# Rows written to DRAM in copies, one of four one-hots on another engine, and two sums in one operation

## The chip, the cores and the metric

The kernel runs on one core of a Trainium2 chip. The metric is the device time of one execution in microseconds (us); lower is better. Before the change three runs gave a median of 2655.18 us (2654.83 to 2657.31). The profile is of one more execution of the same program.

The engines are named as in the profile: PE (TensorE, matrix products), PEld (its weight loads), DVE (VectorE), ACT (ScalarE), POOL (GpSimd) and SP, which here issues transfers only. PEclk is TensorE's granted clock, 1.00 for 2.4 GHz and 0.50 for 1.2 GHz.

## The reference, cut to what matters

One decoder layer for 264 token columns: 256 of a prompt and 8 samples. Mixers give x1; then a layer with 16384 single-neuron experts (PEER) and a second normalization follow:

```python
x1 = layer_norm(ALPHA * x + mix @ w_out, ln1_g, ln1_b)
x2 = layer_norm(ALPHA * x1 + peer(x1, peer_wq, peer_keys1, peer_keys2, peer_u, peer_v), ln2_g, ln2_b)
y = x2 + jax.nn.sigmoid(x2 @ ple_gate_w) * (p @ ple_proj_w)

# in peer, for each token: 8 heads, top 16 of 128x128 key pairs, then
hid = jax.nn.gelu(jnp.einsum('td,thkd->thk', xb, u_tab[ib]), approximate=False)
coef = gb * hid
out = jnp.einsum('thk,thkd->td', coef, v_tab[ib])
```

## The kernel before, in words

**Two ways through the experts.** For 208 of the 264 columns the kernel multiplies with all experts: 128 blocks of `uT` (the u stage, `pair_block` with `u_evac`), a gate matrix that is zero where a token did not choose an expert, and then 8 x 16 blocks of `vP` (the v stage). The other 56 columns take only the expert rows that they chose (`sparse_experts`): 112 indirect gathers of 128 rows of 2048 floats, 56 from `uR` and 56 from `vR`, in groups of 32, 16 and 8 tokens (`GR`). In a group of n tokens each of the 128 partitions serves one token, and each token has 128/n partitions.

**Weights.** Every weight half (128 x 1024 floats, 512 KB) is loaded by SP into one of 5 buffers `w`, rounded by ACT into `whi` (line 146), and its remainder is made by DVE as `wlo` (line 147). Both have 4 buffers and are made 3 halves ahead of PE. A half in the u or v stage is 8 pairs of products (lines 273 or 276, and 274).

**What sets the order.** The program is written out in ticks, one for each half. After each half's products a background scheduler runs tasks as far as a budget allows, and functions that were deferred to this tick. So each engine's order is fixed when the program is built; on the chip each engine works through its own list and waits for semaphores. SP's list has the loads of `w`, the sends of indices (line 1165) and the writes of finished gate blocks `g_d` (line 1205), in one order.

**The rows x1 of the sparse tokens.** `token_rows` transposes the 56 columns of x1 into 56 rows of 8 KB in `xr`, and POOL writes them to DRAM as `x1_d` (line 1227). Before each group `replicate` (lines 1247 to 1251) reads them back so that each partition has the row of its token: one transfer of 1 MB, whose source is written as 128/n copies outermost (with step 0), then n rows, then 2048 floats. DVE multiplies the gathered `uR` rows with it (line 1289); later the same tile collects the `vR` rows (lines 1297, 1299).

**The gate matrix.** `gates` makes for each 4 tokens two one-hot tiles: `o1` by POOL (line 1200, four operations of 128 x 128) and `o2` by ACT. Six ticks later PE multiplies them (line 1213) and ACT copies the product into the gate block `gs`; after 32 tokens SP writes the block to DRAM. A new group of four tokens comes every 3 ticks. On POOL's list the one-hots stand between the gathers (line 1237). A gather waits for the buffer `ug` of the last but one, thus for DVE.

**The second norm.** In class `Norm`, `gather` takes each finished block of 208 columns: DVE subtracts a pilot mean, ACT scales it into `h` and squares it into a block of its own, DVE makes `l` and adds the values (line 847) and the squares (line 848) to two sums. `rest` does the same for the 56 sparse columns, with sums into the last columns of the same two tiles. `stats` multiplies both sums with a constant matrix to sum over partitions (lines 896 and 898).

Of the kernel before, what the change touches and what calls it, by code (L numbers as in the profile page):

```python
# [10 lines left out]
F = mybir.dt.float32  # L11
# [41 lines left out]
def hybrid_step(ctx: ExitStack, tc: tile.TileContext, xT, pT, w_in, w_dt, w_bs, w_bc, w_o, w_q, w_pg, w_pp,  # L53
# [748 lines left out]
    class Norm:  # L802
        def __init__(self, g_base, b_base, name, new, w=T):
            self.g, self.b, self.name, self.new = g_base, b_base, name, new
            self.w = w
            self.h, self.l = [], []
            self.gb = []
            src = cpar[:, g_base:g_base + 32].rearrange("p (a j) -> p j a", a=2)
            h = cpool.tile([128, 16, 2], R, name=name + "gbh")
            l = cpool.tile([128, 16, 2], R, name=name + "gbl")  # L810
            ac.copy(h, src)
            ve.tensor_tensor(l, src, h.bitcast(F), OP.subtract)
            self.gb = [h.bitcast(F), l.bitcast(F)]
            self.s0 = None
            self.c = None
            self.d = []
            self.acc = None
# [8 lines left out]
        def gather(self, s):  # L826
            j = len(self.d)
            w = self.w
            ve.tensor_tensor(s[:, :w], s[:, :w], self.c[:, :w], OP.subtract)
            self.d.append(s)  # L830
            h, l = self.new(self.name)
            q = block("dsq")

            def on_act():
                ac.activation(h[:, :w], s[:, :w], AF.Copy, scale=col(self.g, j))
                ac.activation(q[:, :w], s[:, :w], AF.Square)
                gp.tensor_copy(h[:, T:], self.gb[0][:, j])  # L837
                gp.tensor_copy(l[:, T:], self.gb[1][:, j])
                if j == 0:
                    a = block("da")  # L840
                    gp.tensor_copy(a[:, :w], s[:, :w])
                    self.acc = (a, q)

            def on_dve():
                ve.scalar_tensor_tensor(l[:, :w], s[:, :w], col(self.g, j), h[:, :w].bitcast(F), OP.mult, OP.subtract)
                if j:
                    ve.tensor_tensor(self.acc[0][:, :w], self.acc[0][:, :w], s[:, :w], OP.add)
                    ve.tensor_tensor(self.acc[1][:, :w], self.acc[1][:, :w], q[:, :w], OP.add)

            self.h.append(h)  # L850
            self.l.append(l)
            soon(on_act)
            soon(on_dve)

        def rest(self, xs, sq):
# [9 lines left out]
            yield ("w", 1)  # L865
            ac.activation(sq, xs, AF.Square)
            ve.tensor_reduce(self.acc[0][:, w:T], xs.rearrange("p j t -> p t j"), AX.X, OP.add)
            yield 1.0
            yield ("w", 1)
            ve.tensor_reduce(self.acc[1][:, w:T], sq.rearrange("p j t -> p t j"), AX.X, OP.add)  # L870
            yield 1.0
            for j in range(16):
                while len(self.h) <= j:
# [3 lines left out]
                gp.tensor_copy(self.d[j][:, w:T], x)  # L877
# [14 lines left out]
        def stats(self):  # L892
# [3 lines left out]
            te.matmul(pm[:, :T], o2048, self.acc[0], start=True, stop=True)  # L896
            pv = bank("pv")
            te.matmul(pv[:, :T], o2048, self.acc[1], start=True, stop=True)
# [253 lines left out]
    x1_d = dram.tile([NSP, D], F, name="x1_d")  # L1152
# [34 lines left out]
    def gates(t0, n):  # L1187
        oh = P["oh"]
        grid = Grid()
        for tt in range(t0, t0 + n, 4):  # L1190
# [7 lines left out]
            for q in range(4):  # L1198
                c = slice(tt + q, tt + q + 1)
                gp.tensor_scalar(o1[:, q], iot, slot[0][:, c], slot[2][:, c], OP.is_equal, OP.mult)  # L1200
# [15 lines left out]
    def token_rows():  # L1216
# [10 lines left out]
        gp.dma_start(out=x1_d, in_=xr[:NSP])  # L1227

    def sparse_experts():
# [16 lines left out]
        def replicate(g):  # L1246
            k0, n = GR[g]
            t = lp.tile([128, D], F, name="x1s", tag="x1s", bufs=2)
            gp.dma_start(out=t, in_=bass.AP(tensor=x1_d.tensor, offset=x1_d.offset + k0 * D,
                                            ap=[[0, 128 // n], [D, n], [1, D]]))  # L1250
# [146 lines left out]
    def v_evac(c, db):  # L1397
        def f(ps):
# [5 lines left out]
            if c == ECH - 1:  # L1404
                ve.tensor_tensor(a[:, :TD], a[:, :TD], a[:, TD:], OP.add)
                n2.add(a[:, :T])
# [208 lines left out]
```

## Time and profile before

| | |
|---|---|
| median of three runs | 2655.18 us |
| the profiled execution, its own time | 2653.27 us |
| its span, first to last instruction | 2651.0 us |
| PE busy | 2572.5 us (97%) |
| DVE busy | 2032.7 us (77%) |
| ACT busy | 1426.3 us (54%) |
| POOL busy | 723.4 us (27%) |
| moved by DMA | 692.61 MB, mean 261 GB/s |

The busy share is a mean over the whole span. The u stage lies between about 1140 and 1800 us, the v stage from there to about 2540 us. POOL's share is small in all but high while the gate matrix is made (1290 to 1790 us). A view of stretches (windows) gives for each engine the busy time and, in brackets, how many instructions began; the number of products that PE began in a stretch, against a stretch of the same work where it had no gap, tells how much was lost to gaps and to a lower clock together.

### The profile page before, as it was taken

Reading aid. Unit: us, or ns where it says so; the run is one execution under the profiler, and the core shown is the slowest. Engines: PE = TensorE matmul, PEld = TensorE weight load, DVE = VectorE, ACT = ScalarE, POOL = GpSimd, SP = SyncE. Lnnn points to the kernel's source line nnn. Section 1 sums busy time; section 2 is a strip of 40 time slices with the busy share of each in tenths; the row PEclk is TensorE's granted clock in tenths of the full one; section 3 lists DMA queues with packets and bytes.
Section 4 is the critical chain, followed back from the end, with each engine's and each line's share of the span. In section 5 each row is a group of like instructions: output and inputs, shape, how many; then the busy total and the mean of one; then the engine's idle time right before and its main releaser. Section 6 shows DMA issues by size and latency. Waiting matters only on the chain. (4 is left out here: it accounts for less than half of the span.)

```text
span 2651.0 us, 49042 instructions
## 1 busy us (share of the span) xinstructions
PE 2572.5 (97%) x18985; PEld 2536.4 (96%) x18985; DVE 2032.7 (77%) x3271; ACT 1426.3 (54%) x2170; POOL 723.4 (27%) x775
## 2 busy tenths in 40 slices
PE   8999999999999999999979999799999999999999
PEld 8999999999999999999979899799999999999999
DVE  8899965556445567899878667577889989989986
ACT  5665533454344445654667777675544444445563
POOL 2232200000000010100449689772232233322210
PEclk9999999999999999999989999899999999999999
DMA  6798755555555555566778999899999999999664
GB/s 232 221 294 275 242 169 180 181 173 184 182 180 181 181 178 176 178 198 206 215 249 331 343 341 338 281 353 386 362 348 362 377 355 366 371 358 369 206 196 133
DMA packets 204410, 692.61 MB, mean 261 GB/s; under 512 B 23976, under 2 KB 61528, under 8 KB 188504
## 3 DMA queue, kind: packets, MB, share of 16 engines
q1 hardware_dynamic: 156512, 509.13, 57.5%
q0 software_dynamic: 29648, 162.29, 16.5%
q10 hardware_dynamic: 18016, 18.06, 2.0%
q8 instruction: 148, 2.42, 0.4%
q14 instruction: 86, 0.70, 0.1%
HBM read 649.46 MB, written 39.92 MB: 260 GB/s over the span
## 5 line engine op out<-in xcount | busy, mean ns | idle before, releaser
L147 DVE TENSOR_TENSOR wlo<-w,whi 128x1024 fp32r<-128x1024 f32 x916 | 1117.1, 1225 | 461.8 <-ACT whi L146 449.2
L146 ACT CAST whi<-w 128x1024 fp32r<-128x1024 f32 x916 | 958.9, 1049 | 799.4 <-PE mm L238 289.6
L273 PE MATMUL mm<-x,whi 128*128 128x416 f32 x1920 | 601.7, 373 | 19.0 <-ACT whi L146 19.0
L273 PE MATMUL mm<-co,whi 128*128 128x416 f32 x1920 | 588.4, 367 | 0.9 <-ACT whi L146 0.9
L239 PE MATMUL mm<-x,wlo 128*128 128x264 f32 x1920 | 549.9, 286 | 2.8 <-DVE wlo L147 2.8
L237 PE MATMUL mm<-x,whi 128*128 128x264 f32 x1920 | 549.9, 286 | 1.0 <-ACT whi L146 1.0
L238 PE MATMUL mm<-x,whi 128*128 128x264 f32 x1920 | 547.4, 285 | 0.0
L274 PE MATMUL mm<-x,wlo 128*128 128x208 f32 x2048 | 516.5, 262 | 27.2 <-DVE wlo L147 26.8
L274 PE MATMUL mm<-co,wlo 128*128 128x208 f32 x2048 | 514.4, 261 | 7.9 <-DVE wlo L147 7.6
L274 PEld LDWEIGHTS mm<-x,wlo 128*128 128x128 f32 x2048 | 395.4, 193 | 34.8 <-DVE wlo L147 34.1
L274 PEld LDWEIGHTS mm<-co,wlo 128*128 128x128 f32 x2048 | 390.4, 191 | 15.2 <-DVE wlo L147 14.5
L273 PEld LDWEIGHTS mm<-x,whi 128*128 128x128 f32 x1920 | 366.0, 191 | 24.7 <-ACT whi L146 20.0
L237 PEld LDWEIGHTS mm<-x,whi 128*128 128x128 f32 x1920 | 363.5, 189 | 2.7 <-issue 1.4
L273 PEld LDWEIGHTS mm<-co,whi 128*128 128x128 f32 x1920 | 360.9, 188 | 5.1 <-ACT whi L146 1.8
L239 PEld LDWEIGHTS mm<-x,wlo 128*128 128x128 f32 x1920 | 362.6, 189 | 3.3 <-DVE wlo L147 3.2
L238 PEld LDWEIGHTS mm<-x,whi 128*128 128x128 f32 x1920 | 363.6, 189 | 0.0
L1200 POOL TENSOR_SCALAR o<-iot,slot,slot 128x128 f32<-128x128 f32 x208 | 311.7, 1505 | 3.6 <-ACT slot L1142 1.9
L1237 POOL DMA_INDIRECT ug<-vR,sidx x56 | 101.8, 1818 | 300.8 <-DVE x1s L1299 253.5
L1237 POOL DMA_INDIRECT ug<-uR,sidx x56 | 85.5, 1527 | 227.0 <-DVE ug L1289 202.6
L1299 DVE SCALAR_TENSOR_TENSOR x1s<-ug,scf,x1s 128x2048 f32<-128x2048 f32 x53 | 124.3, 2345 | 16.7 <-DMA ug<-vR,sidx 16.6
L837 POOL CAST r1h<-r1gbh 128x2 fp32r<-128x2 f32 x16 | 5.3, 329 | 476.2 <-PE mm L239 476.2
L1289 DVE SCALAR_TENSOR_TENSOR ug<-ug,x1s 128x2048 f32<-128x2048 f32 x56 | 127.8, 2282 | 3.8 <-DMA ug<-uR,sidx 3.8
(360 smaller groups left out, 3913.2 us busy)
## 6 DMA issues: line engine op xcount, KB each, us to landing
w<-uT SPq DMA_DIRECT2D x256, 512.0 KB
w<-vP SPq DMA_DIRECT2D x256, 512.0 KB
w<-w_in SPq DMA_DIRECT2D x240, 512.0 KB
w<-w_bc SPq DMA_DIRECT2D x32, 512.0 KB
w<-w_bs SPq DMA_DIRECT2D x32, 512.0 KB
w<-w_o SPq DMA_DIRECT2D x32, 512.0 KB
w<-w_q SPq DMA_DIRECT2D x32, 512.0 KB
w<-w_pg SPq DMA_DIRECT2D x32, 512.0 KB
```

Source lines behind the costliest of these rows:

```text
L146: ac.copy(hi, w)
L147: ve.tensor_tensor(lo, w, hi.bitcast(F), OP.subtract)
L237: te.matmul(ps, wh, xh[kb], start=(first and q == 0), stop=False)
L238: te.matmul(ps, wh, xl[kb], start=False, stop=False)
L239: te.matmul(ps, wl, xh[kb], start=False, stop=(last and q == n - 1))
L273: te.matmul(ps, hi[:, ws], xp[kb], start=(kb == 0), stop=False)
L274: te.matmul(ps[:, :TD], lo[:, ws], xp[kb][:, :TD], start=False, stop=False)
L837: gp.tensor_copy(h[:, T:], self.gb[0][:, j])
L1200: gp.tensor_scalar(o1[:, q], iot, slot[0][:, c], slot[2][:, c], OP.is_equal, OP.mult)
L1237: gp.indirect_dma_start(out=t, out_offset=None, in_=tab, in_offset=bass.IndirectOffsetOnAxis(ap=sidx[:, c:c + 1], axis=0))
L1289: ve.scalar_tensor_tensor(t, t, 1.0, x1s, OP.mult, OP.mult, accum_out=shid[:, c:c + 1])
L1299: ve.scalar_tensor_tensor(x1s, t, scf[:, c:c + 1], x1s, OP.mult, OP.add)
```

## The change

Three edits, in four places of the code.

- **Rows in copies.** `x1_d` becomes three DRAM tensors of 128 rows, one for each group. `token_rows` issues three writes, of 32, 16 and 8 rows, each row 4, 8 or 16 times, into the order in which the partitions need them. `replicate` reads 128 rows in their order.
- **One-hots.** Of the four operations for `o1` POOL makes three and DVE the fourth.
- **Second norm.** The squares go into the second half of the same 416 wide tile as the values (where `w < T`, thus in the second norm only), and one operation adds both to one sum. The 56 sparse columns have a sum tile of their own, so that `stats` has four products in place of two. `rest` counts blocks whose operations have been written to the lists (`self.n`) where it counted tiles.

```diff
--- before.py
+++ after.py
@@ -814,6 +814,7 @@
             self.s0 = None
             self.c = None
             self.d = []
+            self.n = 0
             self.acc = None
 
         def pilot(self):
@@ -824,28 +825,39 @@
             self.gather(self.s0)
 
         def gather(self, s):
+
             j = len(self.d)
             w = self.w
+            beside = w < T
             ve.tensor_tensor(s[:, :w], s[:, :w], self.c[:, :w], OP.subtract)
-            self.d.append(s)
+            self.d.append(s[:, :T])
             h, l = self.new(self.name)
-            q = block("dsq")
+            q = s[:, w:2 * w] if beside else block("dsq")
 
             def on_act():
                 ac.activation(h[:, :w], s[:, :w], AF.Copy, scale=col(self.g, j))
-                ac.activation(q[:, :w], s[:, :w], AF.Square)
+                ac.activation(q, s[:, :w], AF.Square)
                 gp.tensor_copy(h[:, T:], self.gb[0][:, j])
                 gp.tensor_copy(l[:, T:], self.gb[1][:, j])
                 if j == 0:
-                    a = block("da")
-                    gp.tensor_copy(a[:, :w], s[:, :w])
-                    self.acc = (a, q)
+                    if beside:
+                        a = lp.tile([128, 2, w], F, name="da", tag="as", bufs=2)
+                        gp.tensor_copy(a.rearrange("p a t -> p (a t)"), s)
+                        self.acc = [(a[:, 0], a[:, 1])]
+                        self.both = a.rearrange("p a t -> p (a t)")
+                    else:
+                        a = block("da")
+                        gp.tensor_copy(a, s)
+                        self.acc = [(a, q)]
 
             def on_dve():
                 ve.scalar_tensor_tensor(l[:, :w], s[:, :w], col(self.g, j), h[:, :w].bitcast(F), OP.mult, OP.subtract)
-                if j:
-                    ve.tensor_tensor(self.acc[0][:, :w], self.acc[0][:, :w], s[:, :w], OP.add)
-                    ve.tensor_tensor(self.acc[1][:, :w], self.acc[1][:, :w], q[:, :w], OP.add)
+                if j and beside:
+                    ve.tensor_tensor(self.both, self.both, s, OP.add)
+                elif j:
+                    for a, x in zip(self.acc[0], (s, q)):
+                        ve.tensor_tensor(a, a, x, OP.add)
+                self.n += 1
 
             self.h.append(h)
             self.l.append(l)
@@ -863,18 +875,20 @@
             ve.tensor_tensor(xs, xs, c[:, None, :].to_broadcast([128, 16, n]), OP.subtract)
             yield 1.0
             yield ("w", 1)
+            a = block("da")[:, 0:2 * n].rearrange("p (a t) -> p a t", a=2)
             ac.activation(sq, xs, AF.Square)
-            ve.tensor_reduce(self.acc[0][:, w:T], xs.rearrange("p j t -> p t j"), AX.X, OP.add)
+            ve.tensor_reduce(a[:, 0], xs.rearrange("p j t -> p t j"), AX.X, OP.add)
             yield 1.0
             yield ("w", 1)
-            ve.tensor_reduce(self.acc[1][:, w:T], sq.rearrange("p j t -> p t j"), AX.X, OP.add)
+            ve.tensor_reduce(a[:, 1], sq.rearrange("p j t -> p t j"), AX.X, OP.add)
+            self.acc.append((a[:, 0], a[:, 1]))
             yield 1.0
             for j in range(16):
-                while len(self.h) <= j:
+                while self.n <= j:
                     yield ("w", 1)
                 h, l, x = self.h[j][:, w:T], self.l[j][:, w:T], xs[:, j]
                 ac.activation(h, x, AF.Copy, scale=col(self.g, j))
-                gp.tensor_copy(self.d[j][:, w:T], x)
+                gp.tensor_copy(self.d[j][:, w:], x)
 
                 def low(h=h, l=l, x=x, j=j):
                     ve.scalar_tensor_tensor(l, x, col(self.g, j), h.bitcast(F), OP.mult, OP.subtract)
@@ -893,9 +907,13 @@
 
             yield ("w", 1)
             pm = bank("pm")
-            te.matmul(pm[:, :T], o2048, self.acc[0], start=True, stop=True)
             pv = bank("pv")
-            te.matmul(pv[:, :T], o2048, self.acc[1], start=True, stop=True)
+            for k, p in enumerate((pm, pv)):
+                t = 0
+                for a in self.acc:
+                    n = a[k].shape[-1]
+                    te.matmul(p[:, t:t + n], o2048, a[k], start=True, stop=True)
+                    t += n
             m = block("m")
             ac.copy(m, pm[:, :T])
             m2 = block("m2")
@@ -1149,7 +1167,7 @@
 
     sx_d = [dram.tile([128, n], U32, name=f"sx{g}_d") for g, (_, n) in enumerate(GR)]
     sg_d = [dram.tile([128, n], F, name=f"sg{g}_d") for g, (_, n) in enumerate(GR)]
-    x1_d = dram.tile([NSP, D], F, name="x1_d")
+    x1_d = [dram.tile([128, D], F, name=f"x1{g}_d") for g in range(len(GR))]
 
     def send(sel, t, nh):
 
@@ -1197,7 +1215,7 @@
             o2 = oh.tile([128, 4, 128], F, name="o2", tag="o2", bufs=3)
             for q in range(4):
                 c = slice(tt + q, tt + q + 1)
-                gp.tensor_scalar(o1[:, q], iot, slot[0][:, c], slot[2][:, c], OP.is_equal, OP.mult)
+                (gp if q < 3 else ve).tensor_scalar(o1[:, q], iot, slot[0][:, c], slot[2][:, c], OP.is_equal, OP.mult)
                 ac.activation(o2[:, q], iot, AF.Abs, bias=slot[1][:, c], scale=-1.0)
             ac.activation(o2, o2, AF.Relu, bias=1.0, scale=-1.0)
             defer(6, lambda o1=o1, o2=o2, gs=gs, q0=q0: g_mm(o1, o2, gs, q0))
@@ -1224,7 +1242,9 @@
                 te.transpose(ps[:NSP, q * 128:(q + 1) * 128], x1sp[:, 4 * b + q], ident)
             ac.copy(xr[:NSP, b * 512:(b + 1) * 512], ps[:NSP])
             yield ("w", 1)
-        gp.dma_start(out=x1_d, in_=xr[:NSP])
+        for g, (k0, n) in enumerate(GR):
+            gp.dma_start(out=x1_d[g].rearrange("(q n) d -> n q d", n=n),
+                         in_=xr[k0:k0 + n, None, :].to_broadcast([n, 128 // n, D]))
 
     def sparse_experts():
         jobs = [(tab, k0, n, c) for k0, n in GR for tab in (uR, vR) for c in range(k0, k0 + n)]
@@ -1244,10 +1264,8 @@
             gp.dma_start(out=scf[:, k0:k0 + n], in_=sg_d[g])
 
         def replicate(g):
-            k0, n = GR[g]
             t = lp.tile([128, D], F, name="x1s", tag="x1s", bufs=2)
-            gp.dma_start(out=t, in_=bass.AP(tensor=x1_d.tensor, offset=x1_d.offset + k0 * D,
-                                            ap=[[0, 128 // n], [D, n], [1, D]]))
+            gp.dma_start(out=t, in_=x1_d[g])
             return t
 
         def folded(g, acc):
@@ -1403,7 +1421,7 @@
                 ve.tensor_tensor(a, ps, a, OP.add)
             if c == ECH - 1:
                 ve.tensor_tensor(a[:, :TD], a[:, :TD], a[:, TD:], OP.add)
-                n2.add(a[:, :T])
+                n2.add(a)
         return f
 
     def finish():
```

The three places in the engines' lists, first POOL's at the start of the gate matrix and of the first sparse group. In the names, `o_` and a number is an `o1` tile, `x_d` the rows in DRAM, `x1s` the tile of replicated rows, `ug` a gathered tile. Before:

```order
L1227 DMA x_d<-xr 56x2048
L1165 DMA sx_d<-ix_16006 32x4x32
...
L1200 TENSOR_SCALAR o_16101<-iot,slot_14373,slot_14375 128x128 x4
L1200 TENSOR_SCALAR o_16209<-iot,slot_14373,slot_14375 128x128 x4
L1200 TENSOR_SCALAR o_16320<-iot,slot_14373,slot_14375 128x128 x4
L1243 DMA sidx<-sx_d 128x32
L1244 DMA scf<-sg_d 128x32
L1237 DMA ug<-uR,sidx 128x2048
L1249 DMA x1s<-x_d 128x1x2048
L1200 TENSOR_SCALAR o_16446<-iot,slot_14373,slot_14375 128x128 x4
```

The same place of POOL's list after the change:

```order
L1246 DMA x_d<-xr 32x4x2048
L1246 DMA x_d<-xr 16x8x2048
L1246 DMA x_d<-xr 8x16x2048
L1183 DMA sx_d<-ix_16010 32x4x32
...
L1218 TENSOR_SCALAR o_16105<-iot,slot_14375,slot_14377 128x128 x3
L1218 TENSOR_SCALAR o_16213<-iot,slot_14375,slot_14377 128x128 x3
L1218 TENSOR_SCALAR o_16324<-iot,slot_14375,slot_14377 128x128 x3
L1263 DMA sidx<-sx_d 128x32
L1264 DMA scf<-sg_d 128x32
L1257 DMA ug<-uR,sidx 128x2048
L1268 DMA x1s<-x_d 128x2048
L1218 TENSOR_SCALAR o_16450<-iot,slot_14375,slot_14377 128x128 x3
```

Three writes stand where one stood, nine one-hots where twelve stood ahead of the index loads and the first gather, and the read of the rows keeps its place.

DVE's list in the middle of the u stage (`as` is a finished u block), before:

```order
L1289 SCALAR_TENSOR_TENSOR ug,shid<-ug,x1s 128x2048
L147 TENSOR_TENSOR wlo<-w,whi 128x1024
L1333 TENSOR_TENSOR as<-mm,as 128x208
L147 TENSOR_TENSOR wlo<-w,whi 128x1024 x2
L1333 TENSOR_TENSOR as<-mm,as 128x208
```

and after:

```order
L1307 SCALAR_TENSOR_TENSOR ug,shid<-ug,x1s 128x2048
L147 TENSOR_TENSOR wlo<-w,whi 128x1024
L1351 TENSOR_TENSOR as<-mm,as 128x208
L147 TENSOR_TENSOR wlo<-w,whi 128x1024
L1218 TENSOR_SCALAR o_19759<-iot,slot_14375,slot_14377 128x128
L147 TENSOR_TENSOR wlo<-w,whi 128x1024
```

One one-hot has come between two remainders `wlo`; there are 52 such places. From the fourth on, this operation has a wait for POOL, because its tile was last written by POOL three groups of tokens earlier.

DVE's list in the second norm, before:

```order
L845 SCALAR_TENSOR_TENSOR r_28010<-acc,cpar,r_28010 128x208
L847 TENSOR_TENSOR da<-da,acc 128x208
L848 TENSOR_TENSOR dsq<-dsq 128x208
L147 TENSOR_TENSOR wlo<-w,whi 128x1024
L1403 TENSOR_TENSOR acc<-mm,acc 128x416
```

and after:

```order
L854 SCALAR_TENSOR_TENSOR r_28014<-acc,cpar,r_28014 128x208
L856 TENSOR_TENSOR da<-da,acc 128x416
L147 TENSOR_TENSOR wlo<-w,whi 128x1024
L1421 TENSOR_TENSOR acc<-mm,acc 128x416
L1423 TENSOR_TENSOR acc<-acc 128x208
```

Two sums of 208 columns have become one of 416; nothing else moved there. SP's list is the same row by row, and PE's differs only in the four products of `stats`.

## Rows read from the trace of the kernel before

**Rows 1.** The page's 40 slices of the span (66 us each): PE's busy tenths and the granted clock.

```profile
PE   8999999999999999999979999799999999999999
PEclk9999999999999999999989999899999999999999
```

**Rows 2.** Stretches around the first sparse group; columns: stretch, its length, then busy us and number begun for PE, PEld, DVE, ACT, POOL, the granted clock, the busy share of the DMA engines and GB/s.

```profile
1282.00:1318.00 36.00, 36.00 (x246) 35.69 (x244) 31.11 (x80) 27.36 (x46) 27.39 (x26) 1.00 0.65 206
1306.00:1312.00 6.00, 6.00 (x43) 5.96 (x43) 5.66 (x18) 5.55 (x10) 5.01 (x6) 1.00 0.11 32
1318.00:1345.00 27.00, 8.88 (x43) 7.89 (x43) 7.56 (x29) 6.62 (x13) 3.27 (x4) 0.62 0.84 193
1318.00:1336.00 18.00, 2.66 (x16) 2.21 (x15) 1.75 (x9) 0.00 (x0) 3.27 (x4) 0.65 1.00 201
1354.00:1363.00 9.00, 7.26 (x38) 6.88 (x38) 8.79 (x16) 4.88 (x11) 1.87 (x2) 0.81 0.57 181
```

**Rows 3.** POOL in order of time around the first sparse group; columns: start, duration, line, operation, output and input, count, and in brackets the idle time before it.

```profile
1297.60 10.01 POOL L1200 TENSOR_SCALAR o<-iot,slot,slot 128x128 f32<-128x128 f32 x6
1307.57 0.63 POOL L1243 DMA_DIRECT2D sidx<-sx_d  x1
1309.73 1.46 POOL L1237 DMA_INDIRECT ug<-uR,sidx  x1 [0.97 <-DMA sidx<-sx_d]
1311.17 0.79 POOL L1249 DMA_DIRECT2D x1s<-x_d  x1
```

**Rows 4.** The same time on ACT and on SP (SPq is the issue of a transfer), same columns.

```profile
1314.08 1.05 ACT L146 CAST whi<-w 128x1024 fp32r<-128x1024 f32 x1
1337.13 1.04 ACT L146 CAST whi<-w 128x1024 fp32r<-128x1024 f32 x1 [22.00 <-DMA w<-uT]
...
1302.64 0.33 SPq L135 DMA_DIRECT2D w<-uT  x1
1316.07 74.48 SPq L135 DMA_DIRECT2D w<-uT  x24
```

**Rows 5.** Stretches around the second sparse group, columns as in rows 2.

```profile
1664.00:1691.00 27.00, 27.00 (x191) 26.87 (x190) 14.28 (x16) 23.59 (x43) 24.34 (x20) 1.00 0.84 260
1691.00:1709.00 18.00, 4.48 (x19) 4.03 (x18) 7.41 (x7) 1.77 (x3) 4.74 (x3) 0.62 0.73 230
1685.00:1697.00 12.00, 6.61 (x47) 6.24 (x45) 0.00 (x0) 6.19 (x11) 3.95 (x5) 0.93 0.96 190
```

**Rows 6.** POOL, then DVE, in order of time around the second sparse group, columns as in rows 3.

```profile
1662.21 18.52 POOL L1200 TENSOR_SCALAR o<-iot,slot,slot 128x128 f32<-128x128 f32 x12
1682.81 1.63 POOL L1237 DMA_INDIRECT ug<-vR,sidx  x1 [0.30 <-issue]
...
1701.59 2.35 DVE L1299 SCALAR_TENSOR_TENSOR x1s<-ug,scf,x1s 128x2048 f32<-128x2048 f32 x1 [16.63 <-DMA ug<-vR,sidx]
```

**Rows 7.** Stretches around the third sparse group, in the v stage, columns as in rows 2.

```profile
2137.00:2164.00 27.00, 27.00 (x182) 26.85 (x181) 20.26 (x23) 9.71 (x10) 8.45 (x10) 1.00 1.02 348
2155.00:2164.00 9.00, 9.00 (x62) 8.95 (x61) 4.75 (x6) 2.10 (x2) 3.11 (x3) 1.00 1.03 260
2164.00:2173.00 9.00, 6.51 (x39) 5.50 (x38) 5.81 (x7) 4.83 (x6) 0.83 (x2) 1.00 1.02 389
```

**Rows 8.** Four shorter gaps of the u stage, columns as in rows 2.

```profile
1396.00:1400.00 4.00, 2.17 (x15) 1.79 (x14) 2.95 (x5) 0.58 (x1) 3.83 (x3) 1.00 0.99 391
1456.00:1464.00 8.00, 6.14 (x29) 5.20 (x28) 2.46 (x4) 4.10 (x9) 7.79 (x8) 0.79 0.32 96
1476.00:1492.00 16.00, 14.19 (x92) 12.81 (x90) 9.83 (x14) 13.37 (x24) 7.38 (x8) 1.00 0.99 385
1616.00:1624.00 8.00, 6.52 (x44) 6.12 (x44) 3.30 (x5) 5.20 (x10) 7.79 (x7) 1.00 0.74 245
```

**Rows 9.** What PE waited for between 1362 and 1680 us: in total, times, the longest.

```profile
PE gps L1213 <- POOL o L1200: 5.0, 6, 1.6
```

**Rows 10.** Groups of instructions by line and shape: busy time and mean ns of one, then the idle time before them.

```profile
L1200 POOL TENSOR_SCALAR o<-iot,slot,slot 128x128 f32<-128x128 f32 x208 | 311.7, 1505 | 3.6 <-ACT slot L1142 1.9
L546 DVE TENSOR_SCALAR arow<-arow,tcol 128x128 f32<-128x128 f32 x64 | 13.6, 283 | 0.0
L1403 DVE TENSOR_TENSOR acc<-mm,acc 128x416 f32<-128x416 f32 x112 | 65.5, 585 | 2.3 <-PE mm L276 2.1
L847 DVE TENSOR_TENSOR da<-da,acc 128x208 f32<-128x208 f32 x15 | 5.5, 366 | 0.0
L848 DVE TENSOR_TENSOR dsq<-dsq 128x208 f32<-128x208 f32 x15 | 5.5, 366 | 0.0
```

**Rows 11.** DMA issues: queue, count, KB of one.

```profile
w<-uT SPq DMA_DIRECT2D x256, 512.0 KB
x1s<-x_d POOLq DMA_DIRECT2D x3, 1024.0 KB
x_d<-xr POOLq DMA_DIRECT2D x1, 448.0 KB
```

**Rows 12.** Stretches after the write of the rows (POOL issued it at 1213.45 us), columns as in rows 2.

```profile
1215.00:1230.00 15.00, 15.00 (x101) 14.90 (x101) 14.48 (x48) 8.27 (x11) 0.00 (x0) 1.00 0.84 268
1245.00:1254.00 9.00, 6.23 (x33) 5.55 (x32) 8.59 (x26) 3.72 (x5) 0.00 (x0) 0.86 0.54 164
```

## The prediction

> **What bounds the kernel now.** I read the page's 40 slices first. PE is at nine tenths or more nearly everywhere; it falls to seven in the 21st and the 26th slice, and there the granted clock falls too [rows 1]. These slices begin at 1325 and 1657 us, both in the u stage. So PE's own work bounds the kernel, plus what PE loses in gaps, and I looked only for those gaps that the change can reach. I count a loss by products begun, since that takes in the slow clock: the number missing against a stretch of the same work without a gap, divided by that stretch's rate.
>
> First sparse group: 246 products in 36 us are 6.83 per us; in 1318 to 1345 there are 43 of 184.5, a loss of 20.7 us [rows 2]. Second: 191 in 27 us are 7.07 per us; 1691 to 1709 has 19 of 127.3, a loss of 15.3 us [rows 5]. Third, in the v stage: 6.74 per us, 39 of 60.7, a loss of 3.2 us [rows 7]. All three follow the read of `x1s`. While it runs the DMA engines are about fully busy and yet carry little: 201 GB/s with 4 copies outermost, 190 with 8, 260 with 16, where other full stretches carry 348 to 391 [rows 2, 5, 7, 8]. A transfer that holds few engines, on which the weight loads then queue, would look like this.
>
> Two delays add to it. In the first group SP issued no weights from 1302.64 to 1316.07, and the DMA engines lay at 0.11 from 1306 to 1312 [rows 2, 4]. POOL reached the index loads only at 1307.57, behind twelve one-hots, and the 1 MB read at 1311.17 [rows 3]. So the gathers and the read missed the empty time and met the weights; ACT then waited 22.00 us for one load [rows 4]. In the second group twelve one-hots took 18.52 us; the gather after them was issued at 1682.81, and DVE stood 16.63 us for it, with `wlo` queued behind [rows 6].
>
> Four shorter gaps of the u stage, by the rate of 7.07, lose 1.9, 3.9, 3.0 and 1.8 us, together 10.6 [rows 8]. POOL is nearly full in three of them, and PE waited 5.0 us for one-hots in six places [rows 8, 9].
>
> **The rows in copies: reads.** The three reads keep their 1 MB [rows 11], but the source is now 128 rows in order, without a copied dimension outermost. I take them to run like a gather of 128 rows. The Trainium skill (DMA: Bandwidth & Descriptors, Rules for kernel authors) says that a leading step-0 dimension of c copies confines a transfer to at most c engines. By that rule the three reads used 4, 8 and at most 16 engines and now use 16; the trace agrees in the order of the losses, 20.7, 15.3 and 3.2 us, though not in the rates of the first two, 201 and 190 GB/s.
>
> **One-hots: POOL.** POOL loses 52 of 208 operations of 1.505 us, 78 us [rows 10]. In the first group nine in place of twelve bring the index loads 4.0 us forward (the last six took 10.01 us, so three take 5.0 at that pace; I take a quarter of the 16 us between the first one-hot and 1307.57). The first gather and the read then start in the empty time. In the second group a quarter of 18.52 us gives 4.6.
>
> First group: weights resume at 1316.07 as before, into nearly free DMA engines. PE had work until about 1320.6 (2.66 us busy after 1318 [rows 2]). If the load lands in 3 to 4 us, the cast (1.04 us [rows 4]) and `wlo` follow at about 1322: 2 us are kept, 18.7 gained. The dip of 1354 to 1363, 23 products or 3.4 us short with DVE 8.79 of 9 us busy [rows 2], is DVE's and stays. Second group: the gather is issued at 1678.2; the read and it are 2 MB, at half of some 350 GB/s [rows 7] 12 us, so DVE goes on at 1690 and PE, dry at 1691.6, lacks about 3 us: 12.3 gained. Third: the same traffic in a full stage; I keep 2, gain 1.2. Of the shorter gaps I take half, 5.3, since only some are POOL's.
>
> **One-hots: DVE.** DVE gains 52 operations. The nearest row is a two-step operation with a column as scalar on 128 x 128, 0.283 us [rows 10]: 14.7 us. Idle time of DVE covers most of it; where it is full (31.11 of 36, 8.79 of 9 [rows 2]) it lands on PE. Below: 0. Above: all 14.7. I take 1.5, about five of them on the path, nearer to zero because most of the 52 lie in stretches like 1664 to 1691, with DVE busy 14.28 of 27 us [rows 5].
>
> **The rows in copies: writes.** 448 KB become 3 MB, on POOL's queue in a row, in a stretch without gathers. From below: zero. The 448 KB passed with 268 GB/s and 101 products in 15 us, no loss [rows 12]. From above: the first group had the same 3 MB on this queue (read and two gathers) and lost 20.7 us. The weights need 512 KB [rows 11] for each half of 16 products, 2.34 us at 6.83 per us, thus 224 GB/s; with 348 in all [rows 7], 3 MB pass in about 25 us beside them, and five buffers plus three halves made ahead cover a delay. DVE, busy 14.48 of 15 us [rows 12], cannot catch up what it misses, and a gap stands already at 1245. I take 3 us, nearer to the row of the same write.
>
> **Second norm.** A pair of sums takes 0.366 + 0.366 us, a 416 wide one 0.585 [rows 10]: 15 x 0.147 = 2.2 us of DVE at most, less as they overlap; bounds 0 and 2.2. `stats` gains two products with the same columns in all. I take a gain of 0.5.
>
> **Sum.** 18.7 + 12.3 + 1.2 + 5.3 + 0.5 = 38.0 gained, 3 + 1.5 = 4.5 paid, net 33.5. From the profiled execution's 2653.27 that gives 2619.8. The median of the runs lies 1.91 above that execution, so 2621.7, forecast 2622 us.
>
> **Rivals.**
>
> *The writes starve the weights.* Their sources lie in 32, 16 and 8 partitions. If they hold few ports or engines, the weight loads queue on these as they did for the read. Price 18 us in place of 3 (mean of 20.7 and 15.3): 2636.7. For it: DVE has no reserve there. Against: 448 KB from 56 partitions passed unseen [rows 12]. The Trainium skill (SBUF — State Buffer, Door 1: The DMA port swizzle) states 189 GB/s for partitions 0 to 31 and 104 for 0 to 15, as few reach few ports. By that page I estimate some 35 us for the three writes, long enough to outlast the buffers; no row here shows it.
>
> *The order of the read was not the cause.* Then 3 MB at once cost what they cost, and only POOL's lead counts: 4.0 + 4.6 + 5.3 + 0.5 = 14.4 less 4.5, so 2645.3. For it: both losses had two gathers beside the read. Against: the rates below 201 at full engines.
>
> *Slower: DVE waits for POOL.* The one-hot on DVE now waits for POOL's writes of the tile's last use, and `wlo` is queued behind it. If each waits for one POOL operation, 52 x 1.505 = 78 us; with half on the path 39.1, so 2660.8. It decides above 39 us on the path, 0.74 us for each. Against: PE reads that tile three ticks before it is reused, and PE's waits for POOL were 5.0 us in 318 [rows 9].
>
> *The gains come back elsewhere*, in a u stage with the same bytes in less time: within 0.2%.
>
> **How the numbers follow.** Forecast 0.62, starved writes 0.16, read order no cause 0.13, slower 0.05, gains given back 0.04. From no change I tell apart 0.2%, about 5.3 us. Faster 0.91 (first three), same 0.04, slower 0.05. Low end: all losses gone and nothing paid, 20.7 + 15.3 + 3.2 + 10.6 + 0.5 = 50.3, so 2604.9. High end: between the second and third case, 2643.
>
> **What would show it.** Right: no PE gap above 3 us around the first two sparse groups, the clock at 1.00 there, the DMA engines carrying over 300 GB/s while `x1s` is read, POOL's one-hots 156 with some 235 us, index loads before 1305. Wrong: ACT waiting for `uT` between 1215 and 1260 with PE idle (the writes), gaps of 10 us after the reads as before (order no cause), DVE one-hots with idle time behind POOL (slower), or the shorter gaps unchanged.

## The result and the profile after

The changed kernel takes 2636.42 us (median of 5 runs, 2632.36 to 2638.41), the kernel before 2654.83 us on the same chip (2648.85 to 2657.31): a ratio of 0.9934 with a 95% interval of 0.9917 to 0.9952. So it is faster, by 18.4 us; the forecast was 2622 us, 32 us less than before. The profiled execution took 2632.36 us with a span of 2630.5 us, 20.5 us less than the span before.

First the slices of the page of the changed kernel, which answer to [rows 1]: PE's busy tenths and the granted clock.

```profile
PE   9999999999999999998999999999999999999999
PEclk9999999999999999999999999999999999999999
```

The two sevens are gone. In their place an eight stands earlier, in the 19th slice, which begins at 1184 us. What happened is read from milestones: the same instruction's start in both traces. These are DVE's rows on the tile `x1s` of the kernel before; the columns are line, operation, output and input, count, shortest, median and longest ns, and the start of the first and of the last in us.

```profile
L1289 DVE SCALAR_TENSOR_TENSOR ug<-ug,x1s x56: 2275/2284/2293, 1358.5 to 2394.7; 128x2048 f32<-128x2048 f32 x56
L1299 DVE SCALAR_TENSOR_TENSOR x1s<-ug,scf,x1s x53: 2339/2344/2352, 1701.6 to 2472.0; 128x2048 f32<-128x2048 f32 x53
L1297 DVE TENSOR_SCALAR x1s<-ug,scf x3: 1286/1286/1353, 1674.4 to 2405.7; 128x2048 f32<-128x2048 f32 x3
```

And of the changed kernel:

```profile
L1307 DVE SCALAR_TENSOR_TENSOR ug<-ug,x1s x56: 2275/2283/2293, 1362.5 to 2375.6; 128x2048 f32<-128x2048 f32 x56
L1317 DVE SCALAR_TENSOR_TENSOR x1s<-ug,scf,x1s x53: 2336/2345/2357, 1685.9 to 2453.6; 128x2048 f32<-128x2048 f32 x53
L1315 DVE TENSOR_SCALAR x1s<-ug,scf x3: 1286/1286/1289, 1670.5 to 2386.6; 128x2048 f32<-128x2048 f32 x3
```

The first multiply of a gathered row starts 4.0 us later than before (1358.5 to 1362.5), although the first read holds PE up far less: between 1318 and 1345 us PE's longest wait is 2.5 us, before it was 17.4. From there the changed kernel gains: it is 3.9 us ahead at the first scaling into `x1s` (1674.4 to 1670.5), 15.7 ahead at the first accumulation (1701.6 to 1685.9), 19.1 ahead at the last multiply, 18.4 at the last accumulation, 20.5 at the end. Each kernel has one trace here, and the five runs of the changed one lie 6 us apart, with its profiled execution the fastest; so a single difference of this kind is known to a few us only. Still, something was lost ahead of 1362 us. The windows of the changed kernel show where (columns as in [rows 2]):

```profile
1180.00:1212.00 32.00, 32.00 (x221) 30.85 (x220) 30.08 (x102) 17.65 (x30) 0.54 (x1) 1.00 0.70 208
1212.00:1275.00 63.00, 47.90 (x260) 44.23 (x259) 43.45 (x133) 20.73 (x29) 1.74 (x3) 0.84 0.75 193
1221.00:1224.00 3.00, 3.00 (x22) 2.98 (x21) 3.00 (x5) 1.31 (x2) 0.00 (x0) 1.00 0.94 115
1230.00:1233.00 3.00, 0.07 (x1) 0.00 (x0) 0.00 (x0) 0.00 (x0) 0.00 (x0) 1.00 0.96 267
1236.00:1239.00 3.00, 3.00 (x12) 2.92 (x12) 2.75 (x15) 0.00 (x0) 0.00 (x0) 0.50 0.84 195
1242.00:1245.00 3.00, 0.00 (x0) 0.00 (x0) 0.00 (x0) 0.00 (x0) 0.00 (x0) 0.80 0.45 142
```

In the same stretch the kernel before began this many products:

```profile
1212.00:1275.00 63.00, 60.23 (x389) 59.06 (x388) 61.00 (x162) 31.36 (x43) 0.58 (x1) 0.97 0.70 214
```

129 products fewer, at 221 in 32 us 18.7 us. The three writes of the rows were issued from 1212.06 us on. At 1221 the DMA engines are 0.94 busy and carry 115 GB/s; at 1230 PE has run dry, and at 1242 PE, DVE and ACT all stand. ACT in order of time (start, duration, operation, in brackets the idle time before it and what ended it) says for what:

```profile
1222.53 0.55 ACT L1354 ACTIVATE as<-as 128x416 f32<-128x416 f32 x1 [0.76 <-DVE as L1351]
1223.11 0.33 ACTq L1355 DMA_DIRECT2D a_d<-as  x1
1233.15 1.04 ACT L146 CAST whi<-w 128x1024 fp32r<-128x1024 f32 x1 [10.08 <-DMA w<-uT]
1234.11 0.33 ACT L1350 COPY as<-mm 128x208 f32<-128x208 f32 x1
1245.14 1.04 ACT L146 CAST whi<-w 128x1024 fp32r<-128x1024 f32 x1 [10.71 <-DMA w<-uT]
1249.00 1.05 ACT L146 CAST whi<-w 128x1024 fp32r<-128x1024 f32 x1 [2.81 <-DMA w<-uT]
```

Three weight loads came late, by 23.6 us in all. This is the sign that the prediction named for the writes. The reads, on the other hand, pass quickly, as forecast; the stretches of [rows 2] and [rows 5] in the changed kernel, with one more of three us inside the first read:

```profile
1318.00:1345.00 27.00, 23.95 (x143) 23.08 (x142) 20.24 (x63) 18.67 (x33) 12.87 (x13) 0.87 0.81 288
1330.00:1333.00 3.00, 3.00 (x23) 2.99 (x22) 0.18 (x1) 0.00 (x0) 1.76 (x2) 1.00 1.02 424
1691.00:1709.00 18.00, 18.00 (x115) 17.86 (x115) 14.29 (x14) 11.38 (x21) 15.60 (x10) 0.91 0.93 357
```

143 products instead of 43 in the first, 115 instead of 19 in the second, and 424 GB/s where full engines carried 201. The rows for the one-hots and the sums (columns as in [rows 10]):

```profile
L1218 POOL TENSOR_SCALAR o<-iot,slot,slot 128x128 f32<-128x128 f32 x156 | 213.9, 1377 | 5.8 <-issue 2.9 <-ACT slot L1160 1.2
L1218 DVE TENSOR_SCALAR o<-iot,slot,slot 128x128 f32<-128x128 f32 x52 | 18.5, 356 | 0.6 <-ACT slot L1160 0.6
L856 DVE TENSOR_TENSOR da<-da,acc 128x416 f32<-128x416 f32 x15 | 8.8, 583 | 0.0
```

POOL is down from 311.7 to 213.9 us for its one-hots (some 235 were forecast). DVE stood 0.6 us in all ahead of its 52 one-hots, and that for ACT's `slot`, not for POOL.

### The profile page after: what moved, and what is told of

Read it like the earlier page. It is cut to its first block, busy times and chain, and to the rows that moved or that the text cites. A ratio compares the mean times of both kernels' runs of the same rounds, so it can differ in the third digit from the quotient of the medians.

```text
span 2630.5 us, 49103 instructions
## 1 busy us (share of the span) xinstructions
PE 2572.6 (98%) x18989; PEld 2536.3 (96%) x18989; DVE 2044.0 (78%) x3308; ACT 1425.5 (54%) x2170; POOL 630.5 (24%) x725
## 4 chain that ended last, share of the span: by engine, by line
PE 76%; DMA 9%; DVE 8%; issue 3%; ACT 2%; POOL 1%; SPq 0%; ACTq 0%; DVEq 0%; POOLq 0%
PE mm L273 18%; PE mm L239 15%; PE mm L237 15%; PE mm L238 15%; PE mm L274 9%; DMA w<-vP 4%; DVE wlo L147 4%; DMA w<-uT 3%; ACT whi L146 1%; PE mm L276 1%; PE gps L1231 1%; POOL o L1218 1%; DVE ug L1307 1%; DVE x1s L1317 1%; DMA ug<-uR,sidx 0%
## 5 line engine op out<-in xcount | busy, mean ns | idle before, releaser
L274 PEld LDWEIGHTS mm<-co,wlo 128*128 128x128 f32 x2048 | 390.4, 191 | 12.5 <-DVE wlo L147 11.8
L1218 POOL TENSOR_SCALAR o<-iot,slot,slot 128x128 f32<-128x128 f32 x156 | 213.9, 1377 | 5.8 <-issue 2.9
L1257 POOL DMA_INDIRECT ug<-uR,sidx x56 | 92.9, 1660 | 271.5 <-DVE ug L1307 232.2
```

What stands on the lines that cost most here:

```text
L274: te.matmul(ps[:, :TD], lo[:, ws], xp[kb][:, :TD], start=False, stop=False)
L1218: (gp if q < 3 else ve).tensor_scalar(o1[:, q], iot, slot[0][:, c], slot[2][:, c], OP.is_equal, OP.mult)
L1257: gp.indirect_dma_start(out=t, out_offset=None, in_=tab, in_offset=bass.IndirectOffsetOnAxis(ap=sidx[:, c:c + 1], axis=0))
```

## The experiments

Theory W: the ordered reads and the shorter queue of POOL gain nearly 40 us, and the three writes, whose sources lie in few partitions, take back about 20 by holding up the weight loads. Rival R: the gain comes from the one-hots, and neither reads nor writes matter. The first four kernels ran on one chip, where before took 2650.44 us (median of 19 runs, 2644.76 to 2661.05).

**The rows alone.** Before, with only this of the change:

```diff
-        gp.dma_start(out=x1_d, in_=xr[:NSP])
+        for g, (k0, n) in enumerate(GR):
+            gp.dma_start(out=x1_d[g].rearrange("(q n) d -> n q d", n=n),
+                         in_=xr[k0:k0 + n, None, :].to_broadcast([n, 128 // n, D]))
...
-            gp.dma_start(out=t, in_=bass.AP(tensor=x1_d.tensor, offset=x1_d.offset + k0 * D,
-                                            ap=[[0, 128 // n], [D, n], [1, D]]))
+            gp.dma_start(out=t, in_=x1_d[g])
```

> Before, with only the rows in copies: three writes of 1 MB and three ordered reads; all one-hots on POOL and the second norm as before. Theory W (the writes starve the weights for some 22 us, and the ordered read runs beside them): a loss at 1215 to 1275 as in the changed kernel, no stretch at 200 GB/s while x1s is read in the first sparse group, but the gather of the second group as late as before, since POOL still has twelve one-hots ahead of it; 2645 to 2657. Rival R (what was gained came from the one-hots, neither reads nor writes matter): 2655, with the losses of 20 and 15 us where they were.

Measured: 2644.22 us, ratio 0.9973 (0.9961 to 0.9986), thus 6.2 us won, a little below W's range. Its windows hold both halves of W:

```profile
1212.00:1275.00 63.00, 46.70 (x252) 42.87 (x251) 41.26 (x127) 19.41 (x27) 0.03 (x1) 0.84 0.76 183
1330.00:1342.00 12.00, 9.46 (x60) 8.60 (x59) 8.00 (x26) 5.72 (x12) 8.14 (x8) 0.97 1.00 400
```

252 products between 1212 and 1275, as few as in the changed kernel, and 400 GB/s while the first read runs. R, which had both losses of before in place, doesn't fit.

**All but the rows.** The changed kernel with the old write and the old read (the lines above, the other way round).

> The changed kernel with the old 448 KB write and the old read (copies outermost): only the one-hots and the norm are left of the change. W: no loss at 1215 to 1240 beyond that of before, but the first read again near 200 GB/s with a gap of 15 us or more behind it; POOL's lead is worth 5 to 14 us, so 2641 to 2650. R (the one-hots are all): 2636, the same as the changed kernel.

Measured: 2642.27 us, ratio 0.9967 (0.9951 to 0.9983): 8.2 us won by the one-hots and the norm together. The loss at 1212 is gone (388 products from 1212 to 1275), and those at the reads are back:

```profile
1312.00:1318.00 6.00, 2.04 (x16) 1.85 (x14) 0.00 (x0) 0.00 (x0) 2.83 (x4) 1.00 0.85 187
1682.00:1688.00 6.00, 0.00 (x0) 0.00 (x0) 0.29 (x1) 1.04 (x1) 0.00 (x0) 0.50 0.67 253
```

Here the first read was issued at 1306.5 us, 4.7 us earlier than before, and PE ran dry all the same, at 187 GB/s. POOL's lead alone doesn't help the read. 6.2 and 8.2 make 14.4; the whole change, on another chip, made 18.4.

**Copies inside the read.** This is the changed kernel with the small write of before. The read of the first two groups runs over the rows first and repeats each inside; the lists of indices and the folding matrix are laid out to match.

```diff
-                                            ap=[[0, 128 // n], [D, n], [1, D]]))
+                                            ap=[[D, n], [0, 128 // n], [1, D]] if g < 2 else
+                                            [[0, 128 // n], [D, n], [1, D]]))
...
-                          ap=[[m, len(src)], [stride, runs], [1, m]]),
+                          ap=[[step, len(src)], [stride, runs], [1, m]]),
...
-                    rows(gp, g, 0, src, m * m, 128 // m, m)
+                    rows(gp, g, 0, src, m if g < 2 else m * m, 128 // m, m, 128 if g < 2 else m)
```

> The changed kernel with the small write of before (448 KB, 56 rows), and the read of the first two groups with the rows outermost and their copies inside; the lists of indices of these two groups are written in the same order, and the folding matrix with them. The third group is read as before, with 16 copies outermost. W: no stall behind the write, and the first two reads at over 300 GB/s: 22 us less than the changed kernel, 2614, between 2608 and 2622. R: 2636. If a read that repeats a row is slow in any order (what helped was the source in 128 rows): 2636 to 2650, with the first read near 200 GB/s.

Measured: 2619.08 us, ratio 0.9873 (0.9851 to 0.9895), the fastest of the four and 23.2 us below the kernel with the copies outermost. By the ratios it lies some 16 us below the changed kernel, where 22 were forecast. In the stretch in which all but the rows had 187 GB/s it carries 352:

```profile
1312.00:1318.00 6.00, 4.49 (x32) 4.27 (x31) 1.02 (x6) 1.52 (x5) 4.06 (x6) 1.00 0.95 352
```

As the base on the two chips of the kernels that follow it gave 0.9863 (0.9846 to 0.9879) and 0.9876 (0.9849 to 0.9904).

> The kernel with the copies inside the read once more, as the base on the same chip for the three that follow: ratio to before 0.985 to 0.989.

> The kernel with the copies inside the read, as the base on the same chip for the three that follow: ratio to before 0.985 to 0.989.

**The writes added to it.** Right behind the small write, the three writes of the changed kernel, to DRAM that nobody reads:

```diff
         gp.dma_start(out=x1_d, in_=xr[:NSP])
+        for g, (k0, n) in enumerate(GR):
+            gp.dma_start(out=xd_d[g].rearrange("(q n) d -> n q d", n=n),
+                         in_=xr[k0:k0 + n, None, :].to_broadcast([n, 128 // n, D]))
```

> The kernel with the copies inside the read, and in addition, right behind the small write, the three writes of 1 MB of the changed kernel, to DRAM that nobody reads. So only the price of the writes is added. W: 18 to 25 us above the kernel without them, near 2636, with ACT waiting for uT some 20 us between 1215 and 1250. Rival (the loss at 1215 to 1275 is DVE's or something else of this stretch): within 5 us of the kernel without them.

Measured: 2640.90 us, ratio 0.9954 (0.9936 to 0.9972), 21.8 us above the same kernel without them. ACT's waits between 1212 and 1275 in that run (total, times, longest):

```profile
ACT whi L146 <- DMA w<-uT: 27.3, 3, 10.8
```

The rival by which the loss there is DVE's falls; the writes have their price, by themselves, in a kernel where nothing else differs.

**Bytes or partitions.** Now 3 MB at the same place in three shapes: from 128 partitions, from 32 (each row four times), from 8 (each row sixteen times). Before took 2651.97 us on this chip, the base with the copies inside the read 2617.52.

```diff
+        for g in range(len(GR)):
+            gp.dma_start(out=xd_d[g], in_=xr)
```

> The kernel with the copies inside the read, and behind its small write three further writes of 1 MB to DRAM that nobody reads, each of 128 partitions by 8 KB (POOL sets the rows tile to zero first, so that all of it is defined). The same bytes in the same place as the writes of the changed kernel, but from all partitions. P (what costs is that the source lies in few partitions): 0 to 5 us above the base. B (3 MB at this place cost it, whatever their shape): about 22 us above the base.

```diff
+        k0, n = GR[0]
+        for x in xd_d:
+            gp.dma_start(out=x.rearrange("(q n) d -> n q d", n=n),
+                         in_=xr[k0:k0 + n, None, :].to_broadcast([n, 128 // n, D]))
```

> The same with the three writes of 1 MB each from 32 partitions, four times each row (three times the first write of the changed kernel). P: less than the changed kernel's 22 us, since its second and third write came from 16 and 8 partitions; 0 to 10 us above the base. B: about 22 us.

The third is the second with `GR[2]` in place of `GR[0]`.

> The same with the three writes of 1 MB each from 8 partitions, sixteen times each row (three times the last write of the changed kernel). P: more than 22 us, 35 to 60 above the base, with weight loads that take over 10 us each while the DMA engines lie half idle. B: about 22 us.

Measured: 2623.13 us from 128 partitions (0.9892, 0.9872 to 0.9912), 2625.06 from 32 (0.9895, 0.9875 to 0.9915), 2663.41 from 8 (1.0036, 1.0023 to 1.0049). Above the base that is 5.6, 7.5 and 45.9 us for the same bytes; the first of these is a little above its forecast, and the first two can't be told apart by their intervals. The same eight us in the three traces, 128 partitions:

```profile
1220.00:1228.00 8.00, 7.75 (x51) 7.08 (x50) 7.72 (x26) 2.26 (x3) 0.00 (x0) 1.00 1.03 420
```

32 partitions:

```profile
1220.00:1228.00 8.00, 8.00 (x55) 7.96 (x54) 5.52 (x14) 1.83 (x3) 0.00 (x0) 1.00 1.00 283
```

8 partitions, and what follows:

```profile
1220.00:1228.00 8.00, 8.00 (x55) 7.96 (x54) 6.70 (x17) 2.88 (x4) 0.00 (x0) 1.00 0.99 71
1228.00:1236.00 8.00, 4.21 (x28) 3.92 (x27) 0.00 (x0) 0.00 (x0) 0.00 (x0) 0.99 0.99 72
1236.00:1244.00 8.00, 0.00 (x0) 0.00 (x0) 0.00 (x0) 0.00 (x0) 0.00 (x0) 0.50 0.95 71
```

At full engines 420, 283 and 71 GB/s. It isn't the bytes. The fewer partitions the source has, the less passes, the weights included: with 8, ACT waited 32.8 us for one load. One part of the expectation misses: the engines were to lie half idle, and they are 0.99 busy.

In these kernels the number of partitions and the size of the outermost dimension of the write change together, and no run varied one alone. The full engines don't tell them apart, since more than one write was in flight. POOL's DMA queue in the run with 8 partitions shows it (packets begun, MB, and the time that they took as a share of 16 engines), from 1220 to 1244 us and from 1262 to 1278:

```profile
q0 software_dynamic: 157, 1.28, 93.2%
q0 software_dynamic: 99, 0.81, 44.8%
```

By 1258 us this queue had carried 2.56 MB, which is the small write and two of the three, so the second line is the third write by itself. Alone it takes a little under half of the engines' time, as the expectation had it. It moves 0.81 MB in 16 us, 51 GB/s; the writes ahead of it, which together held twice that share of the engines, moved 1.28 MB in 24 us, 53 GB/s. So the share of the engines doesn't set the rate here. What all three have in common is the source of 8 partitions, and this speaks for the partitions.

**The read by itself.** Two reads of 1 MB of the first group's rows, behind the small write, where there are no gathers; once with the copies outermost, once with the rows outermost. Before took 2653.41 us here, the base 2623.20.

```diff
+        k0, n = GR[0]
+        for _ in range(2):
+            t = lp.tile([128, D], F, name="xd", tag="x1s", bufs=2)
+            gp.dma_start(out=t, in_=bass.AP(tensor=x1_d.tensor, offset=x1_d.offset + k0 * D,
+                                            ap=[[0, 128 // n], [D, n], [1, D]]))
```

> The base, and right behind its small write two further reads of 1 MB of the first group's 32 rows into tiles that nobody uses, with the 4 copies outermost, as before's read has them. There are no gathers in this stretch, so the read stands alone beside the weights. O (copies outermost hold the engines): 10 to 35 us above the base, with a stretch near or below 210 GB/s at full engines behind 1220. G (the first group's loss came from the read and the gathers together): 0 to 6 us above the base.

> The same two reads with the rows outermost and the copies inside. O: 0 to 6 us above the base, at over 300 GB/s. G: the same as with the copies outermost.

Measured: 2639.45 us with the copies outermost (0.9943, 0.9921 to 0.9964), 2623.89 with the rows outermost (0.9881, 0.9859 to 0.9903): 16.3 and 0.7 us above the base. The same eight us show both, copies outermost and then rows outermost:

```profile
1220.00:1228.00 8.00, 8.00 (x56) 7.95 (x55) 7.76 (x22) 4.17 (x6) 0.00 (x0) 1.00 0.97 136
1220.00:1228.00 8.00, 8.00 (x55) 7.95 (x54) 7.79 (x22) 4.18 (x6) 0.00 (x0) 1.00 0.99 382
```

POOL's queue in these eight us, in the same order:

```profile
q0 software_dynamic: 212, 0.56, 48.2%
q0 software_dynamic: 274, 2.00, 65.0%
```

The trace gives the time from issue to landing, copies outermost (one landing is recorded, that of the second read):

```profile
DMA to landing us min/median/max: 37.5/37.5/37.5
```

Rows outermost (7.2 for the first read, 10.8 for the second):

```profile
DMA to landing us min/median/max: 7.2/9.0/10.8
```

Same rows, same bytes, same tile: for the second read 37.5 us against 10.8, and the slow one holds the weights up as well (ACT waited 24.9 us for `uT` between 1212 and 1275 in the first, 2.4 in the second). G, the read and the gathers together, isn't needed for the first group's loss.

**What is left in the best version.**

```diff
-            defer(2, later_rows)
+            defer(8, later_rows)
...
-            if tab is vR and c == k0 and g + 1 < len(GR):
+            if c == k0 + 3 and g + 1 < len(GR):
                 while g + 1 == len(GR) - 1 and "sent" not in DONE:
                     yield ("w", 1)
                 index(g + 1)
                 xr = replicate(g + 1)
```

(The second block now stands behind the accumulation of a row of v.)

> The base with two places moved: the 16 small sends of the third group's lists, for whose first one SP waits in the first sparse group, six ticks later; and the index loads and the 1 MB read of the next group issued behind the fourth gather of the v part instead of ahead of its second one. In the base some 5 us of products are missing at 1312 to 1324 and some 7 at 1668 to 1680. If both come from transfers that meet there: 4 to 11 us below the base. If the transfers only meet the weights elsewhere: the same within 3 us.

Measured: 2615.74 us, ratio 0.9851 (0.9826 to 0.9875), 7.5 us below the base of its chip, whose interval (0.9849 to 0.9904) it overlaps: lower, but not settled. Its stretches, to be read against the base's, which began 44, 113, 30 and 84 products in them:

```profile
1312.00:1324.00 12.00, 11.66 (x79) 11.00 (x78) 9.68 (x34) 8.98 (x18) 5.50 (x6) 1.00 1.00 387
1324.00:1342.00 18.00, 13.81 (x83) 12.88 (x82) 14.38 (x50) 11.61 (x18) 0.00 (x0) 0.91 0.51 167
1668.00:1680.00 12.00, 12.00 (x83) 11.93 (x83) 9.09 (x11) 9.18 (x18) 11.76 (x8) 1.00 0.95 366
1692.00:1704.00 12.00, 7.53 (x51) 7.23 (x50) 3.18 (x3) 2.52 (x4) 6.44 (x7) 0.95 1.00 418
```

The two holes close and smaller ones open behind them: most of what these moves win is given back in the next window.

## Why the prediction was right and wrong

The sign and the range held (2605 to 2643), and so in the main did the mechanism of the gains. The forecast of 2622 us was 14 us too low, nearly all of it by one term. The measured sizes below are differences of the milestones above, with the scatter said there.

- **Writes: 3 us forecast, 18.7 lost in the profile, 21.8 in the experiment.** This is the step that failed: "I take 3 us, nearer to the row of the same write." The old write [rows 12] was no near row. It is a single 448 KB transfer of 56 partitions, each row once. The new ones send 1 MB each from 32, 16 and 8 partitions, and those from few partitions are what costs: 3 MB from 128 partitions cost 5.6 us, from 8 they cost 45.9. The step that 3 MB pass "in about 25 us beside them" at 348 GB/s took the rate from a stretch whose transfers reach all partitions; the engines were full at 115. With five buffers and three halves made ahead PE ran until 1230, 18 us after the writes were issued, and then twice dry. The rival "The writes starve the weights" was the case that came, at 18 us in place of 3 and 2636.7 in all, with a chance of 0.16. The Trainium skill (SBUF — State Buffer, Door 1: The DMA port swizzle) was the rule that spoke against the change, and the trace agrees with its order: 283 GB/s with a source of 32 partitions, weights included, 71 with 8. My estimate from that page, 35 us for the three writes, was the better sum: the last late load was cast at 1249.00, 37 us after the first issue.
- **First group: 18.7 forecast.** The start of the first multiply went from 18.7 us behind to 4.0 behind: 14.7 gained. Index loads "before 1305" didn't come, they were issued at 1321.16, since the writes had moved all of this stretch back; in the kernel with all but the rows they were issued at 1301.69. The 424 GB/s while `x1s` is read came as named (over 300). Of the gaps above 3 us none stood there, PE's longest wait being 2.5 us, but the clock was 0.87 and not 1.00: 143 products in 27 us are 41.5 short of 184.5, 6.1 us.
- **Second group: 12.3 forecast, 11.8 gained** (3.9 to 15.7 ahead); DVE's wait for the gather went from 16.63 us [rows 6] to 4.9. The same two milestones, the first scaling and the first accumulation, show a gain of 8.9 us in the kernel with the rows alone and a loss of 0.5 in the one with all but the rows. So this gain is the read's; POOL's lead alone gave nothing here.
- **Shorter gaps: 5.3 forecast, 7.9 gained** between the first multiply (4.0 behind) and the first scaling (3.9 ahead); PE's wait for one-hots went from 5.0 us [rows 9] to 0.2. Between the same milestones the kernel with all but the rows gained 9.5 us and the one with the rows alone lost 1.9, so it was the one-hots.
- **Third group: 1.2 forecast; norm: 0.5.** From 15.7 ahead to 19.1 at the last multiply are 3.4 us, over the end of the u stage and most of the v stage. The last 1.4 up to the end hold the norm, which no run took alone; its operation took 583 ns where I said 585.
- **DVE's one-hots: 1.5 forecast.** One took 356 ns where I took 283, thus 18.5 us in place of 14.7. What of it lay on the path isn't separated: it is inside the gains above and inside the 8.2 us of the kernel with all but the rows. My terms for that kernel make 4.0 + 4.6 + 5.3 + 0.5 - 1.5 = 12.9; the measured 8.2 has this just inside its interval (0.9951 is 13.0 us). Its trace is 14.4 us ahead of before's at the first scaling and 11.7 at the end, so there some of the gain came back later on.

The gains sum to 14.7 + 11.8 + 7.9 + 3.4 + 1.4 = 39.2 us, less 18.7 for the writes 20.5; forecast were 38.0 less 1.5 for DVE, 36.5. So all but the writes came within 3 us in sum, which is as near as single traces can tell.

"The order of the read was not the cause" falls: by itself the order is worth 37.5 against 10.8 us to the landing of the second read, and two extra reads cost 16.3 against 0.7 us. My read share was 18.7 + 12.3 less POOL's 4.0 + 4.6, thus 22.4; the order of the first two reads, with the lists laid out to match, gave 23.2; that they agree this closely is luck, for the intervals of the two kernels leave several us either way. Of the Trainium skill's rule on copies outermost (DMA: Bandwidth & Descriptors, Rules for kernel authors) the result holds: the same copies inside cost nothing that the runs can tell. The trace names no single engine, but the share of POOL's queue fits the rule too: two reads of 4 copies in flight took 48.2% of the time of 16 engines, as much as eight of them have, and with the rows outermost 65.0%. "DVE waits for POOL" falls with 0.6 us of waiting in 52 operations, and "the gains come back elsewhere" with the milestones, which grow after 1362 us but for 0.7 us between the last multiply and the last accumulation.

## What to carry to other kernels

When a transfer is reshaped to make a later one cheap, price its own shape too: how many partitions its source has, and which dimension is outermost, before the bytes. Here the repetition cost nothing that could be measured as an inner dimension of the read, while moving it into a write from 8 to 32 partitions gave half of the gain back. And a row of the profile bounds a new transfer only if it has its shape; where the nearest row differs in that, the forecast belongs between the bounds rather than at the low one.

## What the runs showed that I had not expected

Engines at 0.99 that carry 71 GB/s: writes from 8 partitions, more than one in flight, kept the 16 DMA engines busy and let hardly any weights by. A busy share near 1 says that packets are under way, not that bytes move; the two columns have to be read together.

A stall costs more than its length. In the changed kernel PE stood from 1230 to 1233 (one product in 3 us), and when work came back the clock granted was 0.50, the 1.2 GHz level: 12 products in the three busy us from 1236, where 22 are usual.
